# RMS norms around the MLP of a hybrid decoder layer: weight product ahead of the root, part transposes earlier, h read back by plain loads

## The chip, the cores and the metric

The kernel runs on one core of a Trainium2 chip. The core has a matrix engine (TensorE, PE in the rows), a vector engine (VectorE, DVE), an activation engine (ScalarE, ACT), a general engine (GpSimd, POOL) and queues that issue transfers between memory and the on-chip buffer (SyncE's queue is called SPq, GpSimd's own POOLq). The engines run side by side and each works through its own instructions strictly in the order in which they stand; they meet only at semaphores. The metric is the device time of one execution in microseconds (us); lower is better.

## The reference, cut to what matters

```python
def rms_norm(x, w):
    xf = x.astype(jnp.float32)
    y = xf * lax.rsqrt(jnp.mean(xf * xf, axis=-1, keepdims=True) + RMS_EPS)
    return (y * w.astype(jnp.float32)).astype(x.dtype)
...
        mix = jnp.concatenate([o_gdn, o_moba], axis=-1) @ w_out[i]
        h = h + rms_norm(mix, attn_post_norm[i])
        f = jnp.square(jax.nn.relu(rms_norm(h, mlp_pre_norm[i]) @ w_up[i])) @ w_down[i]
        h = h + rms_norm(f, mlp_post_norm[i])
        h = h + jax.nn.sigmoid(h @ w_ple_gate[i]) * (p[i] @ w_ple[i])
```

There are 512 rows of width 1024, and the MLP is 4096 wide. Everything is in 32-bit floats.

## The kernel before

The 512 rows are four tiles of 128 rows (t = 0 to 3). Every large product is made of three matmuls on operands split in a rounded part and a remainder (`mm3`, lines 188 and 191): ACT casts the rounded part ("h" or the first `sr` of a pair), DVE subtracts it for the remainder ("l", or the second `sr`). A weight block goes from a DMA into a slab `sf`, from there by an ACT cast (line 681) and a DVE subtraction (line 682) into two slabs `sr`.

Two places of the program matter here.

The first lies between the attention and the MLP. `po` is the product of the mixed heads with `w_out`, in two halves of 512 columns. The first half of all four tiles is done at once and copied to `h_t[t]` (line 706). The second half is done tile after tile: 24 matmuls for a tile, then its norms. ACT sums the squares of the half (`pn1t`), GpSimd adds the two halves' sums, scales them and takes the power -0.5 (`norm_r`, lines 674, 154 and 155), DVE multiplies by the root and the norm's weight (line 736, two halves) and adds x (line 737, two halves). That is h. ACT sums its squares (`mn0t`, `mn1t`), GpSimd takes the second root, and DVE makes the MLP's input `xr` (line 740). h is stored to memory (`hd`, line 741). PE then transposes `xr` in eight blocks (line 212, names `u`), and ACT and DVE split the result into `u2Th` and `u2Tl` (lines 203 and 204). The transposes of tiles 0 and 1 stand inside the `po` matmuls of tiles 2 and 3. Right behind the `po` of tile 3 come the first products of the MLP, `pu`, on columns 0 to 255, which are tiles 0 and 1; the transposes of tiles 2 and 3 stand inside these.

The second place is the end of the MLP. The last quarter of the down projection (`pd`) is added to sums (`done`, line 904), a norm follows (`qn`, line 909), h is added by an accumulating DMA from GpSimd's queue (line 913; for tile 3 by DVE, line 911), and PE transposes the result (line 892) for the gate product `pg`. Between the two places the MLP keeps PE at work with products of 5 us each.

The order on each engine is made by a scheduler from the order of the code and from ranks; a block under `tc.high_priority(n)` is ranked n places ahead. DMAs issued by the SP queue start in order: one that waits holds those behind it. Slabs are taken from and given back to a list, so the order of `take` and `give` decides which slab a load uses, and with it what it waits for.

Of the kernel before, what the change touches and what calls it, by code (L numbers as in the profile page):

```python
# [12 lines left out]
ALU = mybir.AluOpType  # L13
# [4 lines left out]
NT = T // P  # L18
D = 1024
# [50 lines left out]
def hybrid_layer(ctx: ExitStack, tc: tile.TileContext, x, p, w_in, w_tok, w_out, w_up, w_down, w_ple, w_gate,  # L70
# [33 lines left out]
    def j4(ap):  # L104
        return ap.rearrange("p (j c) -> p j c", j=4)
# [97 lines left out]
        nc.scalar.copy(dst[0], src)  # L203
        nc.vector.tensor_sub(dst[1], src, dst[0].bitcast(F32))  # L204

    def transpose_in(u, dst, t, name):

        for q in range(2):
            pt = ptr(f"{name}{t}_{q}")
            for i in range(4):  # L210
                k = 4 * q + i
                nc.tensor.transpose(pt[:, i * P:(i + 1) * P], u[:, k * P:(k + 1) * P], ident)
            s = (slice(None), slice(4 * q, 4 * q + 4), slice(t * P, (t + 1) * P))
            put_split((dst[0][s], dst[1][s]), j4(pt))


    uT = split_big("uT")
# [453 lines left out]

    def norm_r(ss, name):
        r = m_.tile([P, 1], F32, tag="nr", bufs=4, name=f"{name}r")
        nc.gpsimd.tensor_add(r, ss[:, 0:1], ss[:, 1:2])
        rsqrt(r, r, 1.0 / D, 1)
        return r

    def split(src):
# [24 lines left out]
            out_proj(pts[t], t, k)  # L703
    for t in range(NT):
        pt = pts[t]
        nc.vector.tensor_copy(h_t[t][:, hf(0)], pt)
        sum_half(pt, po_ss[t][:, 0:1], f"pn0{t}")
    wo = load_rows(w_out[:, hf(1)], "wo1", (4, 6, 0, 2))
    xrs = []
# [13 lines left out]
    for t in range(NT):  # L723
        xr = take()
        nc.sync.dma_start(xr, x[tk(t), :])
        pt = pany(f"po1{t}")
        for k in ks:
            out_proj(pt, t, k)
            if t > 1 and k == ks[2 + t]:
                transpose_in(xrs[t - 2], u2T, t - 2, "u2")  # L730
        sum_half(pt, po_ss[t][:, 1:2], f"pn1{t}")
        r = norm_r(po_ss[t], f"pn{t}")
        ss = ss_tile(f"mn{t}")
        for i, src in enumerate((h_t[t][:, hf(0)], pt)):
            hh = h_t[t][:, hf(i)]
            nc.vector.scalar_tensor_tensor(hh, src, r, nw[0][:, hf(i)], op0=ALU.mult, op1=ALU.mult)
            nc.vector.tensor_add(hh, hh, xr[:, hf(i)])
            sum_half(hh, ss[:, i:i + 1], f"mn{i}{t}")
        r = norm_r(ss, f"mn{t}")
        nc.vector.scalar_tensor_tensor(xr, h_t[t], r, nw[1], op0=ALU.mult, op1=ALU.mult)  # L740
        nc.sync.dma_start(hd[tk(t), :], h_t[t])
        give(h_t[t])
        xrs.append(xr)
# [137 lines left out]
    C = ((sums[2], sums[3]), (sums[6], sums[5]))  # L881
    done = [[two(C[t // 2][i])[:, t % 2] for i in range(2)] for t in range(NT)]
    h2T = split_big("h2T")

    h_last = take()
    nc.sync.dma_start(h_last, hd[tk(NT - 1), :])

    def transpose_done(t):
        for q in range(2):
# [6 lines left out]
    for t in range(NT):  # L896
        ss = ss_tile(f"qn{t}")
        for i in range(2):
            pt = pany(f"pd{t}_{i}")
            for n, (r, k) in enumerate((r, k) for r in range(2) for k in range(PAIRS)):  # L900
                mm3(pt, (f_hl[k][0][:, r, tk(t)], f_hl[k][1][:, r, tk(t)]), wd[r, i][k], n == 0, n == 2 * PAIRS - 1)
                if i == 0 and n == 3 and t > 1:
                    transpose_done(t - 2)
            add(done[t][i], done[t][i], pt)
            sum_half(done[t][i], ss[:, i:i + 1], f"qn{i}{t}")

        r = norm_r(ss, f"qn{t}")
        for i in range(2):
            nc.vector.scalar_tensor_tensor(done[t][i], done[t][i], r, nw[0][:, hf(i)], op0=ALU.mult, op1=ALU.mult)
            if t == NT - 1:  # L910
                add(done[t][i], done[t][i], h_last[:, hf(i)])
            else:
                nc.gpsimd.dma_start(done[t][i], hd[tk(t), hf(i)], accum_op=ALU.add)


    late = [nw[0], h_last]
    for i in range(2):
        if i == 1:

# [65 lines left out]
```

## Time and profile before

| | |
|---|---|
| median of 3 runs | 696.54 us (695.7 to 697.95) |
| the profiled execution, its own time | 696.68 us |
| its span, first to last instruction | 694.9 us |
| PE busy | 680.2 us, 98% |
| DVE, ACT, POOL busy | 439.0, 323.8 and 46.5 us |
| bytes read from and written to memory | 70.51 and 7.08 MB |

A row of the timeline gives the start in the span, the duration, the engine, the line, the operation with the tile written and the tiles read, the shape and the count; in brackets stands how long the engine had been idle before it and what ended that. Where several instructions are merged, the duration is from the first start to the last end. An instruction starts somewhat before the one ahead of it has left its engine, so starts lie closer than durations. Durations of matmuls are modelled, their starts are recorded.

### The profile page before, as it was taken

The numbers are of one execution on the slowest core, as the hardware profiler recorded it, in microseconds if no ns is written. First come the engines' busy times: TensorE is split into PE (matmuls) and PEld (weight loads), VectorE is DVE, ScalarE is ACT, GpSimd is POOL, SyncE is SP. The second block draws the span as 40 slices with busy tenths as digits, with TensorE's granted clock in tenths as the row PEclk, the third lists the DMA queues.
The fourth block names the chain that finished last, engine by engine and source line by source line (L and its number), as shares of the span: only waits on it lengthen the run. The fifth ranks groups of instructions, "written<-read, shape, count | busy, mean of one in ns | idle before, by whom it ended". The sixth has DMA issues, their size and how long they took to land.

```text
span 694.9 us, 8996 instructions
## 1 busy us (share of the span) xinstructions
PE 680.2 (98%) x3418; PEld 565.6 (81%) x3418; DVE 439.0 (63%) x689; ACT 323.8 (47%) x598; POOL 46.5 (7%) x89
## 2 busy tenths in 40 slices
PE   8999999999999999979999999999999999999997
PEld 5998888888877768879888888888888888778886
DVE  4748889367676656574476347966579668545632
ACT  6536343433466655345356544644444444532311
POOL 1401100000011100320000000000000000032000
PEclk9999999999999999989999999999999999999999
DMA  8731323532112018368003441054301032644431
GB/s 332 303 122 62 103 86 102 116 110 92 31 31 62 31 62 287 126 211 315 31 31 113 160 134 49 31 160 143 122 31 60 31 121 79 196 105 71 155 109 46
DMA packets 38412, 79.24 MB, mean 114 GB/s; under 512 B 9760, under 2 KB 10400, under 8 KB 38368
## 3 DMA queue, kind: packets, MB, share of 16 engines
q1 hardware_dynamic: 36784, 75.51, 33.4%
q0 software_dynamic: 864, 1.57, 1.6%
q10 hardware_dynamic: 720, 1.57, 0.6%
q8 instruction: 27, 0.44, 0.2%
q14 instruction: 17, 0.14, 0.1%
HBM read 70.51 MB, written 7.08 MB: 112 GB/s over the span
## 4 chain that ended last, share of the span: by engine, by line
PE 88%; DMA 3%; DVE 3%; ACT 3%; issue 2%; POOL 1%; POOLq 0%; ACTq 0%; DVEq 0%
PE pu L191 17%; PE pd L191 13%; PE pu L188 8%; PE pd L188 6%; PE pc L191 6%; PE pg L191 4%; PE pc L188 3%; PE po L191 3%; PE pg L188 2%; PE pmk L191 2%; PE pmq L191 2%; PE wv L191 2%; PE pz L191 2%; PE po L188 1%; PE pav L596 1%
## 5 line engine op out<-in xcount | busy, mean ns | idle before, releaser
L191 PE MATMUL pd<-sr,sr 128*128 128x512 f32 x464 | 143.5, 390 | 0.5 <-DVE sr L682 0.5
L191 PE MATMUL pu<-u2Tl,sr 128*128 128x512 f32 (+1 forms) x288 | 106.2, 369 | 1.7 <-DVE u2Tl L204 1.7
L188 PE MATMUL pu<-u2Th,sr 128*128 128x512 f32 (+1 forms) x288 | 106.0, 370 | 1.9 <-ACT u2Th L203 1.9
L191 PE MATMUL pu<-u2Th,sr 128*128 128x512 f32 (+1 forms) x288 | 106.0, 369 | 0.0
L191 PEld LDWEIGHTS pd<-sr,sr 128*128 128x128 f32 x464 | 86.9, 188 | 19.5 <-DVE sr L682 1.6
L188 PE MATMUL pd<-sr,sr 128*128 128x512 f32 x232 | 90.7, 391 | 0.5 <-ACT sr L681 0.5
L682 DVE TENSOR_TENSOR sr<-sf,sr 128x1024 fp32r<-128x1024 f32 x48 | 58.3, 1221 | 33.8 <-PE pd L191 13.8
L682 DVE TENSOR_TENSOR sr<-wd,sr 128x1024 fp32r<-128x1024 f32 x42 | 51.2, 1221 | 28.5 <-PE pu L191 27.1
L779 ACT ACTIVATE f<-pu 128x512 f32<-128x512 f32 (+1 forms) x36 | 19.9, 551 | 97.9 <-PE pu L191 97.9
L188 PEld LDWEIGHTS pu<-u2Th,sr 128*128 128x128 f32 x288 | 55.1, 192 | 11.1 <-ACT u2Th L203 2.3
L191 PEld LDWEIGHTS pu<-u2Tl,sr 128*128 128x128 f32 x288 | 55.3, 192 | 10.8 <-DVE u2Tl L204 2.0
L191 PEld LDWEIGHTS pu<-u2Th,sr 128*128 128x128 f32 x288 | 55.3, 192 | 8.6
L681 ACT CAST sr<-sf 128x1024 fp32r<-128x1024 f32 x48 | 50.2, 1046 | 25.3 <-DMA sf<-in_w_down 8.9
L681 ACT CAST sr<-wd 128x1024 fp32r<-128x1024 f32 x42 | 44.1, 1050 | 19.4 <-PE pd L191 19.4
L188 PEld LDWEIGHTS pd<-sr,sr 128*128 128x128 f32 x232 | 43.6, 188 | 10.2 <-ACT sr L681 1.3
L188 PE MATMUL pc<-uTh,w_h 128*128 128x512 f32 x96 | 39.0, 407 | 0.0
L191 PE MATMUL pc<-uTh,w_l 128*128 128x512 f32 x96 | 38.4, 400 | 0.0
L191 PE MATMUL pc<-uTl,w_h 128*128 128x512 f32 x96 | 38.2, 398 | 0.0
L833 DVE TENSOR_TENSOR sf<-sf,pd 128x512 f32<-128x512 f32 x28 | 19.0, 683 | 22.2 <-PE pd L191 22.2
L838 DVE TENSOR_TENSOR wd<-wd,wd 128x1024 f32<-128x1024 f32 x24 | 29.3, 1223 | 0.6
L188 PE MATMUL pg<-sr,h2Th 128*128 128x512 f32 (+1 forms) x72 | 26.5, 368 | 0.0
L191 PE MATMUL pg<-sr,h2Th 128*128 128x512 f32 (+1 forms) x72 | 26.3, 366 | 0.0
(422 smaller groups left out, 1318.6 us busy)
## 6 DMA issues: line engine op xcount, KB each, us to landing
sf<-in_w_up SPq DMA_DIRECT2D x32, 512.0 KB, 3.3
wd<-in_w_down SPq DMA_DIRECT2D x24, 512.0 KB, 4.3
w_r<-in_w_in SPq DMA_DIRECT2D x12, 512.0 KB, 3.6
wo_r<-in_w_out SPq DMA_DIRECT2D x8, 512.0 KB, 3.8
sf<-in_w_ple_gate SPq DMA_DIRECT2D x8, 512.0 KB, 3.9
sf<-in_w_down SPq DMA_DIRECT2D x8, 512.0 KB, 4.3
wv_r<-in_w_tok SPq DMA_DIRECT2D x4, 520.0 KB, 6.4
x<-in_x SPq DMA_DIRECT2D x4, 512.0 KB, 6.8
```

Of the source, the lines that this page charges most:

```text
L188: nc.tensor.matmul(dst, l[0], r[0], start=start, stop=False)
L191: nc.tensor.matmul(dst, a, b, start=False, stop=stop and i == 1)
L596: nc.tensor.matmul(po[:, j * P:], mov[:, j, tk(h)], PT[:, j, j * P:], start=j == 0, stop=j == 3)
L681: nc.scalar.copy(hi, src)
L682: nc.vector.tensor_sub(lo, src, hi.bitcast(F32))
L779: nc.scalar.activation(fq[:, side, c0:c1], pt[:, :n], AF.Relu)
L833: add(dst, dst, pts[j])
L838: sub(B[dst + (kk,)], B[x_ + (kk,)], B[y_ + (kk,)])
```

## The change

In `norm_r` GpSimd prepares the sum of the first half ahead, DVE adds the second half's sum to it in one small operation, and GpSimd takes the power. The product with the norm's weight is taken out of the operation that multiplies by the root: it is made from the raw product ahead of the root, for the first half of `po` in place of the copy, and the operation behind the root multiplies by the root and adds x (or h) at once. `xr` is made in two halves. The transposes of tiles 0 and 1 stand one and two steps of three matmuls earlier, and their split parts are ranked 60 places ahead. At the end of the MLP, h is read back for all four tiles by plain loads of 512 KB on the SP queue, and no DMA accumulates. In the changed kernel lines up to 203 keep their numbers; the norm's weight product of the second half stands on line 735, the operation behind the root on 739, `xr` on 743, the small operation of `norm_r` on 676.

```diff
--- before.py
+++ after.py
@@ -203,7 +203,7 @@
         nc.scalar.copy(dst[0], src)
         nc.vector.tensor_sub(dst[1], src, dst[0].bitcast(F32))
 
-    def transpose_in(u, dst, t, name):
+    def transpose_in(u, dst, t, name, ahead=0):
 
         for q in range(2):
             pt = ptr(f"{name}{t}_{q}")
@@ -211,7 +211,8 @@
                 k = 4 * q + i
                 nc.tensor.transpose(pt[:, i * P:(i + 1) * P], u[:, k * P:(k + 1) * P], ident)
             s = (slice(None), slice(4 * q, 4 * q + 4), slice(t * P, (t + 1) * P))
-            put_split((dst[0][s], dst[1][s]), j4(pt))
+            with tc.high_priority(ahead):
+                put_split((dst[0][s], dst[1][s]), j4(pt))
 
 
     uT = split_big("uT")
@@ -671,8 +672,9 @@
 
     def norm_r(ss, name):
         r = m_.tile([P, 1], F32, tag="nr", bufs=4, name=f"{name}r")
-        nc.gpsimd.tensor_add(r, ss[:, 0:1], ss[:, 1:2])
-        rsqrt(r, r, 1.0 / D, 1)
+        nc.gpsimd.tensor_scalar(r, ss[:, 0:1], 1.0 / D, EPS, op0=ALU.mult, op1=ALU.add)
+        nc.vector.scalar_tensor_tensor(r, ss[:, 1:2], 1.0 / D, r, op0=ALU.mult, op1=ALU.add)
+        nc.gpsimd.tensor_tensor(r, r, half[:, :1], op=ALU.pow)
         return r
 
     def split(src):
@@ -703,7 +705,7 @@
             out_proj(pts[t], t, k)
     for t in range(NT):
         pt = pts[t]
-        nc.vector.tensor_copy(h_t[t][:, hf(0)], pt)
+        nc.vector.tensor_mul(h_t[t][:, hf(0)], pt, nw[0][:, hf(0)])
         sum_half(pt, po_ss[t][:, 0:1], f"pn0{t}")
     wo = load_rows(w_out[:, hf(1)], "wo1", (4, 6, 0, 2))
     xrs = []
@@ -726,18 +728,19 @@
         pt = pany(f"po1{t}")
         for k in ks:
             out_proj(pt, t, k)
-            if t > 1 and k == ks[2 + t]:
-                transpose_in(xrs[t - 2], u2T, t - 2, "u2")
+            if t > 1 and k == ks[3]:
+                transpose_in(xrs[t - 2], u2T, t - 2, "u2", 60)
         sum_half(pt, po_ss[t][:, 1:2], f"pn1{t}")
         r = norm_r(po_ss[t], f"pn{t}")
+        nc.vector.tensor_mul(h_t[t][:, hf(1)], pt, nw[0][:, hf(1)])
         ss = ss_tile(f"mn{t}")
-        for i, src in enumerate((h_t[t][:, hf(0)], pt)):
+        for i in range(2):
             hh = h_t[t][:, hf(i)]
-            nc.vector.scalar_tensor_tensor(hh, src, r, nw[0][:, hf(i)], op0=ALU.mult, op1=ALU.mult)
-            nc.vector.tensor_add(hh, hh, xr[:, hf(i)])
+            nc.vector.scalar_tensor_tensor(hh, hh, r, xr[:, hf(i)], op0=ALU.mult, op1=ALU.add)
             sum_half(hh, ss[:, i:i + 1], f"mn{i}{t}")
         r = norm_r(ss, f"mn{t}")
-        nc.vector.scalar_tensor_tensor(xr, h_t[t], r, nw[1], op0=ALU.mult, op1=ALU.mult)
+        for i in range(2):
+            nc.vector.scalar_tensor_tensor(xr[:, hf(i)], h_t[t][:, hf(i)], r, nw[1][:, hf(i)], op0=ALU.mult, op1=ALU.mult)
         nc.sync.dma_start(hd[tk(t), :], h_t[t])
         give(h_t[t])
         xrs.append(xr)
@@ -881,9 +884,9 @@
     C = ((sums[2], sums[3]), (sums[6], sums[5]))
     done = [[two(C[t // 2][i])[:, t % 2] for i in range(2)] for t in range(NT)]
     h2T = split_big("h2T")
-
-    h_last = take()
-    nc.sync.dma_start(h_last, hd[tk(NT - 1), :])
+    h_in = [take() for t in range(NT)]
+    for t in range(NT):
+        nc.sync.dma_start(h_in[t], hd[tk(t), :])
 
     def transpose_done(t):
         for q in range(2):
@@ -906,14 +909,14 @@
 
         r = norm_r(ss, f"qn{t}")
         for i in range(2):
-            nc.vector.scalar_tensor_tensor(done[t][i], done[t][i], r, nw[0][:, hf(i)], op0=ALU.mult, op1=ALU.mult)
-            if t == NT - 1:
-                add(done[t][i], done[t][i], h_last[:, hf(i)])
-            else:
-                nc.gpsimd.dma_start(done[t][i], hd[tk(t), hf(i)], accum_op=ALU.add)
-
-
-    late = [nw[0], h_last]
+            nc.vector.tensor_mul(done[t][i], done[t][i], nw[0][:, hf(i)])
+        for i in range(2):
+            nc.vector.scalar_tensor_tensor(done[t][i], done[t][i], r, h_in[t][:, hf(i)], op0=ALU.mult, op1=ALU.add)
+        if t < NT - 1:
+            give(h_in[t])
+
+
+    late = [nw[0], h_in[NT - 1]]
     for i in range(2):
         if i == 1:
 
```

On PE the transposes of tile 1 (`u_0`, `u_1`, from the slab with tile 1's `xr`) stand inside the `po` of tile 3. Before:

```order
L191 MATMUL po_3012<-wo_6_h,mx3l 128x512
L188 MATMUL po_3012<-wo_0_h,mg0h 128x512
L191 MATMUL po_3012<-wo_0_l,mg0h 128x512
L191 MATMUL po_3012<-wo_0_h,mg0l 128x512
L188 MATMUL po_3012<-wo_0_h,mg1h 128x512
L191 MATMUL po_3012<-wo_0_l,mg1h 128x512
L191 MATMUL po_3012<-wo_0_h,mg1l 128x512
L212 MATMUL u_0_3031<-ident,sf_2659 128x128 x4
L212 MATMUL u_1_3038<-ident,sf_2659 128x128 x4
```

And in the changed kernel:

```order
L188 MATMUL po_3012<-wo_6_h,mx3h 128x512
L191 MATMUL po_3012<-wo_6_l,mx3h 128x512
L191 MATMUL po_3012<-wo_6_h,mx3l 128x512
L212 MATMUL u_0_3025<-ident,sf_2659 128x128 x4
L212 MATMUL u_1_3032<-ident,sf_2659 128x128 x4
L188 MATMUL po_3012<-wo_0_h,mg0h 128x512
```

They moved ahead of six matmuls. Those of tile 0, inside the `po` of tile 2, moved ahead of three.

On DVE, between the `xr` of tile 1 (`sf_2659`) and the split parts of tile 1 (`u2Tl` from `u_0` and `u_1`), the rows before were:

```order
L740 SCALAR_TENSOR_TENSOR sf_2659<-sf_2656,mn1r,sf_2654 128x1024
L204 TENSOR_TENSOR u2Tl<-u_0_2967,u2Th 128x4x128
L204 TENSOR_TENSOR u2Tl<-u_1_2974,u2Th 128x4x128
L736 SCALAR_TENSOR_TENSOR sf_2657<-sf_2657,pn2r,sf_2653 128x512
L736 SCALAR_TENSOR_TENSOR sf_2657<-po_2951,pn2r,sf_2653 128x512
L737 TENSOR_TENSOR sf_2657<-sf_2657,sf_2660 128x512 x2
L682 TENSOR_TENSOR sr_2673<-sf_2663,sr_2672 128x1024
L740 SCALAR_TENSOR_TENSOR sf_2660<-sf_2657,mn2r,sf_2654 128x1024
L204 TENSOR_TENSOR u2Tl<-u_0_3031,u2Th 128x4x128
L204 TENSOR_TENSOR u2Tl<-u_1_3038,u2Th 128x4x128
```

`sf_2657` is h of tile 2, `sf_2660` its `xr`, and `sr_2673` the remainder of a weight block of `w_up` that is loaded into the slab `sf_2663`. In the changed kernel:

```order
L743 SCALAR_TENSOR_TENSOR sf_2659<-sf_2656,mn1r,sf_2654 128x512
L204 TENSOR_TENSOR u2Tl<-u_0_2964,u2Th 128x4x128
L204 TENSOR_TENSOR u2Tl<-u_1_2971,u2Th 128x4x128
L743 SCALAR_TENSOR_TENSOR sf_2659<-sf_2656,mn1r,sf_2654 128x512
L676 SCALAR_TENSOR_TENSOR pn2r<-pn2s,pn2r 128x1
L735 TENSOR_TENSOR sf_2657<-po_2951,sf_2653 128x512
L739 SCALAR_TENSOR_TENSOR sf_2657<-sf_2657,pn2r,sf_2660 128x512 x2
L684 TENSOR_TENSOR sr_2673<-sf_2663,sr_2672 128x1024
L676 SCALAR_TENSOR_TENSOR mn2r<-mn2s,mn2r 128x1
L743 SCALAR_TENSOR_TENSOR sf_2660<-sf_2657,mn2r,sf_2654 128x512
L204 TENSOR_TENSOR u2Tl<-u_0_3025,u2Th 128x4x128
L204 TENSOR_TENSOR u2Tl<-u_1_3032,u2Th 128x4x128
```

The split parts moved between the halves of `xr`. The weight block's remainder stays between the norms of tile 2, and on ACT the order of this stretch is unchanged: sum of squares of `po` of tile 2, cast of the weight block in `sf_2663`, the two sums of squares of h of tile 2, the two casts `u2Th` of tile 1.

On the SP queue, from the load of the last norm's weight on, the loads of the changed kernel stand in this order (`hd` is h, `ple` the embedding's product; before, the slab `sf_3077` took a block of `w_ple_gate`, `sf_2653` and `sf_2654` took parts of `ple`, and behind the last `w_down` block came one load of `hd` and two of `w_ple_gate`):

```order
L889 DMA sf_3077<-hd 128x1024
L692 DMA sf_2659<-in_w_down 128x2x512
L692 DMA sf_2662<-in_w_ple_gate 128x2x512
L692 DMA sf_2653<-in_w_ple_gate 128x2x512
L692 DMA sf_2660<-in_w_down 128x2x512
L932 DMA sf_2662<-ple 128x512
L692 DMA sf_2661<-in_w_down 128x2x512
L692 DMA sf_2659<-in_w_down 128x2x512
L692 DMA sf_2654<-in_w_ple_gate 128x2x512
```

Two blocks of `w_ple_gate` moved from behind the eight `w_down` blocks to between them; the three other loads of `hd` stand where these were.

## Rows read from the trace of the kernel before

**Rows 1.** The page: engines with their busy time (share of the span) and instructions.

```profile
PE 680.2 (98%) x3418; PEld 565.6 (81%) x3418; DVE 439.0 (63%) x689; ACT 323.8 (47%) x598; POOL 46.5 (7%) x89
```

**Rows 2.** Who waited for whom, TensorE's waits: us in total, times, longest.

```profile
PE pu L188 <- ACT u2Th L203: 1.9, 1, 1.9
PE pu L191 <- DVE u2Tl L204: 1.7, 1, 1.7
...
PE pd L188 <- ACT sr L681: 0.5, 1, 0.5
PE pd L191 <- DVE sr L682: 0.5, 1, 0.5
PE h L892 <- DMA sf<-hd: 0.5, 1, 0.5
```

**Rows 3.** Busy time by stretch: length, then PE, PEld, DVE, ACT and POOL busy (instructions), the granted TensorE clock, the DMA engines' share, GB/s.

```profile
236.00:244.00 8.00, 6.58 (x33) 4.85 (x31) 4.64 (x20) 6.11 (x24) 2.40 (x4) 1.00 0.00 1
...
298.00:303.00 5.00, 1.66 (x8) 0.88 (x6) 3.95 (x5) 2.99 (x8) 2.05 (x5) 0.81 0.60 206
303.00:308.00 5.00, 4.69 (x22) 4.69 (x23) 4.51 (x7) 1.77 (x3) 0.55 (x1) 0.51 0.99 336
308.00:312.00 4.00, 4.00 (x36) 4.00 (x36) 1.33 (x2) 2.07 (x5) 0.93 (x3) 1.00 0.41 136
340.00:590.00 250.00, 250.00 (x1105) 206.96 (x1104) 166.74 (x162) 123.23 (x148) 0.00 (x0) 1.00 0.28 88
```

**Rows 4.** The timeline of TensorE, at one wait of an earlier stage and around the end of `po`.

```profile
239.41 0.30 PE L592 MATMUL prt<-ident,pr 128*128 128x128 f32 x1 [1.22 <-DVE pr L589]
...
288.32 0.39 PE L191 MATMUL po<-wo_h,mx3l 128*128 128x512 f32 x1
...
294.66 0.39 PE L191 MATMUL po<-wo_h,mx3l 128*128 128x512 f32 x1
...
298.38 0.40 PE L191 MATMUL po<-wo_h,mg3l 128*128 128x512 f32 x1
300.68 0.89 PE L188 MATMUL pu<-u2Th,sr 128*128 128x256 f32 x4 [1.91 <-ACT u2Th L203]
303.31 0.58 PE L191 MATMUL pu<-u2Tl,sr 128*128 128x256 f32 x1 [1.75 <-DVE u2Tl L204]
...
307.95 0.28 PE L191 MATMUL pu<-u2Tl,sr 128*128 128x256 f32 x1
```

**Rows 5.** The norms of tile 0 on the timelines of ACT, POOL and DVE.

```profile
280.64 0.60 ACT L667 ACTIVATE pn10j<-po 128x512 f32<-128x512 f32 x1 [1.62 <-PE po L191]
...
281.41 0.19 POOL L674 TENSOR_TENSOR pn0r<-pn0s 128x1 f32<-128x1 f32 x1 [38.38 <-ACT pn10j L667]
...
281.97 0.56 POOL L155 TENSOR_TENSOR pn0r<-pn0r,half 128x1 f32<-128x1 f32 x1
...
282.56 0.75 DVE L736 SCALAR_TENSOR_TENSOR sf<-sf,pn0r,sf 128x512 f32<-128x512 f32 x1 [2.44 <-POOL pn0r L155]
...
283.89 1.28 DVE L737 TENSOR_TENSOR sf<-sf,sf 128x512 f32<-128x512 f32 x2
287.38 1.28 DVE L740 SCALAR_TENSOR_TENSOR sf<-sf,mn0r,sf 128x1024 f32<-128x1024 f32 x1 [2.20 <-POOL mn0r L155]
```

**Rows 6.** Small operations of an earlier stage: one on DVE, and the one on POOL that takes its result.

```profile
237.27 0.15 DVE L567 TENSOR_TENSOR so<-so,rq 128x4 f32<-128x4 f32 x1
...
237.59 0.19 POOL L154 TENSOR_SCALAR so<-so 128x4 f32<-128x4 f32 x1 [26.39 <-ACT pr L587]
```

**Rows 7.** From tile 1 to the split parts of tile 1 that the first `pu` reads: rows of ACT, DVE, SPq and POOL.

```profile
286.18 0.60 ACT L667 ACTIVATE pn11j<-po 128x512 f32<-128x512 f32 x1
...
293.81 0.61 ACT L667 ACTIVATE pn12j<-po 128x512 f32<-128x512 f32 x1
...
296.31 1.05 ACT L681 CAST sr<-sf 128x1024 fp32r<-128x1024 f32 x1 [1.80 <-DMA sf<-in_w_up]
298.68 0.63 ACT L667 ACTIVATE mn02j<-sf 128x512 f32<-128x512 f32 x1 [1.32 <-DVE sf L737]
...
299.11 1.21 DVE L682 TENSOR_TENSOR sr<-sf,sr 128x1024 fp32r<-128x1024 f32 x1
301.37 1.28 DVE L740 SCALAR_TENSOR_TENSOR sf<-sf,mn2r,sf 128x1024 f32<-128x1024 f32 x1 [1.05 <-POOL mn2r L155]
302.57 1.28 DVE L204 TENSOR_TENSOR u2Tl<-u,u2Th 128x512 fp32r<-128x512 f32 x2
...
285.20 7.15 SPq L741 DMA_DIRECT2D hd<-sf  x2
292.39 0.44 SPq L718 DMA_DIRECT2D sf<-in_w_up  x1
...
294.59 0.93 POOL L674 TENSOR_TENSOR pn2r<-pn2s 128x1 f32<-128x1 f32 x1 [0.44 <-ACT pn12j L667]
```

**Rows 8.** The page's DMA issues: KB of one, median us from issue to landing.

```profile
sf<-in_w_up SPq DMA_DIRECT2D x32, 512.0 KB, 3.3
...
x<-in_x SPq DMA_DIRECT2D x4, 512.0 KB, 6.8
...
sf<-ple SPq DMA_DIRECT2D x7, 256.0 KB, 2.7
```

**Rows 9.** The timeline of DVE at the end of the MLP: three remainders of `w_down` blocks.

```profile
596.37 3.50 DVE L682 TENSOR_TENSOR sr<-sf,sr 128x1024 fp32r<-128x1024 f32 x3 [4.22 <-PE pu L191]
```

## The prediction

> **What bounds the kernel now.** I read the engines' busy time first: TensorE has work for 98% of the span [rows 1], and through the whole MLP, from 340 to 590 us, it never pauses [rows 3]. So what shortens the kernel is a pause of TensorE, or time that it runs at its lower clock. The list of its waits comes next. Its two longest stand at the first MLP products: 1.9 us for `u2Th` and 1.7 us for `u2Tl`. At the end of the MLP there are three of 0.5 us, two for `w_down` weights and one for the accumulating DMA of h [rows 2]. Then the stretches: between 303 and 308 us the granted clock is 0.51 (the lower level, 1.2 GHz), and 22 matmuls take 5 us, while from 308 us on 36 take 4 us at 1.00 (2.4 GHz), 0.111 us each [rows 3]. TensorE's timeline puts it together: the last matmul of `po` starts at 298.38, so the first `pu` could start 0.23 later, at 298.61 (24 matmuls of `po` and 1 us of transposes lie between 288.32 and 294.66); the 26th `pu` matmul starts at 307.95 [rows 4]. At full clock without a wait, 25 steps of 0.111 bring it at 301.4. About 6.5 us are lost there: the waits, and the clock that fell in them. That is what the change can win at the first place. At the second it is mainly the 0.5 us wait for the DMA.
>
> **The change part by part, first place.** I carry the new order through with the durations of rows, and take 0.1 us for a hand-over that no row shows (rows 5 and 6 show 0.03 to 0.17).
>
> The root. Before: from the first GpSimd operation (281.41) to the DVE operation that uses the root (282.56), 1.15 us [rows 5]. Now: a DVE operation of 0.15, a hand-over of 0.17 [rows 6], the power of 0.56 and 0.03 to DVE [rows 5]: 0.91. The product of `po` with the weight lies under the power; its cost is that of the copy or multiply it replaces. Behind the root two operations replace four: the first half of h is there 0.75 after the root, the second 0.67 later (half the distance of 282.56 and 283.89 [rows 5]).
>
> Tile 0: the sum of squares starts at 280.64 and hands over at 281.41, so 0.77 a sum [rows 5]. Root 282.32, halves of h at 283.07 and 283.74, sums from 283.17 to 284.71, second root 285.62, `xr` in halves at 286.37 and 287.04, in place of 288.66 (287.38 and 1.28 [rows 5]). TensorE reaches the transposes at 288.55, right behind the matmul of 288.32 [rows 4]: no wait.
>
> Tile 1: its `po` sum starts at 286.18 at the latest [rows 7]. Root 287.86, h at 288.61 and 289.28, sums to 290.25, second root 291.16, first half of `xr` 291.91. Now DVE does both split parts of tile 0 (1.28 [rows 7]) before the second half of `xr`, so that is there at 293.8. TensorE wants it behind the matmul of 294.66, at 294.89 [rows 4]: 1.1 us to spare. This cover is thin: if the chain of tile 1 is later by more than that, `po` stalls for the rest.
>
> Tile 2: `po` is done about 292.4. The small operation stands behind the second half of `xr`, 293.8; root 294.7; h at 295.5 and 296.1. On ACT a weight cast stands ahead of the sums of h, and waits for its load. Its issue stands on the SP queue behind the store of h of tile 1, at 292.39 before [rows 7], now near 289.7 (h of tile 1 complete at 289.28; transposes of tile 0 done at 289.6). The load took 3.9 us (292.39 to 296.31 [rows 7]), so it lands at 293.6, the cast ends at 294.65, and the sums start at 295.6, held by h alone, and end at 297.1. On DVE the weight remainder of 1.21 [rows 7] runs to 297.3.
>
> Here one price is uncertain. A GpSimd operation of 0.19 took 0.93 beside a DVE operation on tiles of the buffer [rows 5, 7], so I let GpSimd's preparation of `mn2r` wait until the remainder ends and be done at 297.45: small operation 297.5, root 298.4, first half of `xr` 299.1, first split part of tile 1 at 299.7. The power of `pn1r` and `pn2r` runs beside the product of `po` with the weight (0.64 to 0.69 as the other operations that read `po` or `u` [rows 7]); no row shows that pair. It costs nothing, or, held until the product ends, up to 0.45 each. I take nothing, since the held one of rows 7 stood beside an operation with all inputs in the buffer.
> The Trainium skill (SBUF — State Buffer, Who interferes with whom) states that DVE contends with GpSimd when it has two inputs in SBUF, and not with one input there and one in PSUM. By it the power is not held here, but the weight product at the end of the MLP, with both inputs in SBUF, does hold it; the sum would stay, since a whole tile of `pd` stands between that norm and its transposes.
>
> TensorE therefore starts `pu` at 298.61, its second matmul needs the remainder of tile 1 and starts at 299.8: one wait of 1.2 us instead of 1.9 and 1.7. A wait of 1.22 us at 239.41 left the clock at 1.00 [rows 3, 4]. With the clock kept, the 26th matmul starts at 299.8 and 24 times 0.111, at 302.5 in place of 307.95: 5.5 us won. Tiles 2 and 3 follow a chain of the same shape and TensorE wants them only 36 and 84 `pu` matmuls on, 4 and 9 us later; the weights of the next products were loaded far ahead. From there TensorE is never idle until 590 us, and everything else waits for it, so the 5.5 us stay.
>
> **Second place.** With h read by plain loads, tile 0 needs one operation behind the root instead of that and a DMA; the wait of 0.47 to 0.5 us [rows 2] goes. The three loads of h stand where two `w_ple_gate` loads and one of h stood, behind the last `w_down`, so they land while the products of tiles 1 and 2 still run, ahead of the transposes of tile 0. The two `w_ple_gate` loads moved between the `w_down` loads: some 512 KB more are ahead of the last of these. Cost: nothing if the remainders of `w_down` go on waiting for TensorE, as the three at 596.37 do after 4.2 us of idle DVE [rows 9]; above, 256 KB more cost 0.6 us each (3.3 against 2.7 us to land [rows 8]), so 1.2 us on the two 0.5 us waits for weights. Below nothing: those two could go, a gain of 1.0. I take nothing, being nearest to rows 9. The four more DVE multiplications and the two earlier casts fall where both engines wait for TensorE.
>
> **Sum.** 5.5 and 0.5, 6.0 us: the profiled execution goes from 696.68 to 690.7. It lies 0.1 above the median of 696.54, so I say 690.6.
>
> **Rivals.**
> *The clock falls all the same.* The stretch from 298 us has a clock of 0.81, though TensorE did four matmuls between its waits [rows 3, 4]. So little idle time was enough; against it stands the 1.22 us wait that left the clock alone. The 22 matmuls at half clock took 4.64 us (303.31 to 307.95 [rows 4]) in place of 2.44: 2.2 us are not won, 692.8.
> The Trainium skill (TensorE: Matmul & The Clock Gate, HAM oscillation — how this bites in real kernels) says that a pause for data can throttle TensorE, and that every such pause is paid for again in slow matmuls. Rows 3 agree, 0.51 behind the pause. By it this rival holds if the pause left is still long enough.
> *The weight cast holds the norm (the slower side).* ACT works in order, so the sums of h of tile 2 can't start before the cast of the `w_up` block, and its load now decides as soon as it lands 0.9 us later than worked out (sums ready at 295.6 less the cast's 1.05, 294.5). From there each us costs one. At a landing 4.4 us late, near 298, `u2Tl` is as late as before; with the clock fallen too the place gains nothing, and slower by 0.3% (2.1 us) needs a landing at 300.6, 11 us after the issue. For it: before, ACT stood 1.80 us for this load [rows 7]. Against: the longest median of a 512 KB load is 6.8 us, and of these 3.3 [rows 8]. At 6.8 us the loss is 2.0 us plus the clock's 2.2: 694.8. At 11 us, 698.7 or more.
> *The loads of `w_ple_gate` delay the last `w_down` blocks.* The bound above: 691.8. Against it stand rows 9.
> *Nothing moves.* If DVE, POOL and ACT hand over so slowly that three engines in the root cost what two did, 0.24 us a root comes back. Four roots lie on the path: 691.6, no more.
>
> **How the numbers follow.** My forecast (waits of 0.6 to 1.8 us at `pu`, the clock kept, the second place between 0 and 1 us): 0.62, 689.3 to 691.8. The clock falls: 0.15, 692.8. `w_down` late, or slow roots: 0.08, about 691.7. The cast holds: 0.10, from 692 to 699, of that half above 694.5. Something I have not seen: 0.05. All waits gone at both places would be 688.6. The range is 688.6 to 694.2. A difference of 0.3% (2.1 us) is about what a measurement of this kernel tells from none, so faster ends at 694.4: the first three cases and half of the fourth with some of the fifth, 0.87; same 0.07; slower 0.06.
>
> **What would show it right or wrong.** Right: TensorE's waits list one wait for `u2Tl` of about 1.2 us and none for `u2Th`; the stretch behind it has a clock of 1.00; the weight cast on ACT starts near 293.6 and the sums of tile 2 near 295.6; no transposes wait inside `po`; no wait for h at the end, the two waits for `w_down` still at 0.5. Wrong: a clock near 0.5 behind the first `pu`; a wait of the transposes near 294.9; ACT idle for a DMA ahead of the sums of tile 2; waits for `w_down` above 1 us. If the two places together give less than 2 us, my picture of the first place is wrong.

## The result, and the profile after

The changed kernel takes 690.13 us (median of 5 runs, 689.76 to 690.44) against 696.59 us before (5 runs, 695.70 to 697.95): a ratio of 0.9905, 95% interval 0.9891 to 0.9920. Its profiled execution has a span of 688.1 us, 6.8 us less than the 694.9 of before. Of that, 6.0 us had been forecast. Two executions of the experiments, 2959.63 us of e2_end and 1377.37 us of e5_early, are left out of every time and ratio below.

The page, engines' busy time, to be read against [rows 1]: TensorE is busy for 3.6 us less with the same 3418 instructions. Of this, 2.4 us lie between the last `po` matmul and the first of the last down products (294.3 before, 291.9 after), mainly matmuls that no longer run at half clock; 0.95 lies in the first 20 us (17.86 before, 16.91 after), ahead of the change.

```profile
PE 676.6 (98%) x3418; PEld 563.2 (82%) x3418; DVE 442.6 (64%) x707; ACT 323.7 (47%) x598; POOL 39.3 (6%) x71
```

TensorE's waits after (us in total, times, longest), in place of [rows 2]. The wait for `u2Th` is gone, that for `u2Tl` is 0.5 us, no wait for h is left, and those for `w_down` (line 684 and 683) are still there:

```profile
PE pd L191 <- DVE sr L684: 0.7, 2, 0.5
PE pu L191 <- DVE u2Tl L204: 0.5, 1, 0.5
...
PE pd L188 <- ACT sr L683: 0.3, 1, 0.3
```

The stretches of [rows 3] (length, then PE, PEld, DVE, ACT, POOL busy, granted clock, DMA share, GB/s). The clock is 1.00 throughout, where before it was 0.81 and 0.51:

```profile
298.00:303.00 5.00, 4.53 (x36) 4.18 (x35) 4.94 (x9) 2.81 (x7) 0.73 (x2) 1.00 0.98 317
303.00:308.00 5.00, 5.00 (x45) 5.00 (x44) 3.42 (x6) 2.63 (x6) 1.24 (x2) 1.00 0.98 320
```

TensorE's timeline around the end of `po`, and where the last down products (`pd`) begin, and the transposes behind the first of them, as in [rows 4]. The row at 302.12 is the 26th `pu` matmul:

```profile
298.17 0.39 PE L191 MATMUL po<-wo_h,mg3l 128*128 128x512 f32 x1
298.40 0.28 PE L188 MATMUL pu<-u2Th,sr 128*128 128x256 f32 x1
299.15 0.38 PE L191 MATMUL pu<-u2Tl,sr 128*128 128x256 f32 x1 [0.47 <-DVE u2Tl L204]
299.37 0.28 PE L191 MATMUL pu<-u2Th,sr 128*128 128x256 f32 x1
...
302.12 0.28 PE L191 MATMUL pu<-u2Tl,sr 128*128 128x256 f32 x1
...
590.55 0.39 PE L188 MATMUL pd<-sr,sr 128*128 128x512 f32 x1
...
617.37 1.03 PE L895 MATMUL h<-ident,sf 128*128 128x128 f32 x8
618.15 0.48 PE L188 MATMUL pd<-sr,sr 128*128 128x512 f32 x1
```

And the same last rows before:

```profile
596.34 0.39 PE L188 MATMUL pd<-sr,sr 128*128 128x512 f32 x1
...
624.16 0.63 PE L892 MATMUL h<-ident,sf 128*128 128x128 f32 x4 [0.47 <-DMA sf<-hd]
624.54 0.48 PE L188 MATMUL pd<-sr,sr 128*128 128x512 f32 x1
```

From the last `po` matmul to the first of the last down products it is 292.38 us after and 297.96 before: 5.58 us won at the first place. From there to the matmul behind the transposes 27.60 and 28.20: 0.60 at the second. The last matmul of the program is followed by 4.42 us in place of 4.80 (below), and `po` itself ended 0.21 earlier, for a reason ahead of the change.

The chain of tile 2 that the prediction worked out, on ACT, DVE, POOL and the SP queue, against [rows 7]:

```profile
293.36 1.05 ACT L683 CAST sr<-sf 128x1024 fp32r<-128x1024 f32 x1 [0.35 <-DMA sf<-in_w_up]
295.06 0.63 ACT L668 ACTIVATE mn02j<-sf 128x512 f32<-128x512 f32 x1 [0.65 <-DVE sf L739]
...
292.73 0.74 DVE L743 SCALAR_TENSOR_TENSOR sf<-sf,mn1r,sf 128x512 f32<-128x512 f32 x1
...
295.54 1.22 DVE L684 TENSOR_TENSOR sr<-sf,sr 128x1024 fp32r<-128x1024 f32 x1
296.84 0.16 DVE L676 SCALAR_TENSOR_TENSOR mn2r<-mn2s,mn2r 128x1 f32<-128x1 f32 x1
297.74 0.75 DVE L743 SCALAR_TENSOR_TENSOR sf<-sf,mn2r,sf 128x512 f32<-128x512 f32 x1 [0.74 <-POOL mn2r L677]
298.41 1.28 DVE L204 TENSOR_TENSOR u2Tl<-u,u2Th 128x512 fp32r<-128x512 f32 x2
...
295.94 0.87 POOL L675 TENSOR_SCALAR mn2r<-mn2s 128x1 f32<-128x1 f32 x1 [1.76 <-ACT mn02j L668]
...
289.52 0.33 SPq L720 DMA_DIRECT2D sf<-in_w_up  x1
```

The reader sees two things: ACT's cast no longer decides (h comes 0.65 us behind it), and DVE stands idle for 0.74 us for the root, one operation ahead of the split parts of tile 1 (`u2Tl`) that TensorE waits for.

### The profile page after: what moved, and what is told of

It is laid out like the page before. It is cut to its first block, busy times and chain, and to the rows that moved or that the text cites. A ratio compares the mean times of both kernels' runs of the same rounds, so it can differ in the third digit from the quotient of the medians.

```text
span 688.1 us, 8994 instructions
## 1 busy us (share of the span) xinstructions
PE 676.6 (98%) x3418; PEld 563.2 (82%) x3418; DVE 442.6 (64%) x707; ACT 323.7 (47%) x598; POOL 39.3 (6%) x71
## 4 chain that ended last, share of the span: by engine, by line
PE 88%; DMA 3%; ACT 3%; DVE 3%; issue 1%; POOL 1%; ACTq 0%; DVEq 0%; POOLq 0%
PE pu L191 16%; PE pd L191 14%; PE pu L188 8%; PE pd L188 7%; PE pc L191 6%; PE pg L191 4%; PE pc L188 3%; PE po L191 3%; PE pg L188 2%; PE pmk L191 2%; PE pmq L191 2%; PE wv L191 2%; PE pz L191 2%; DMA sf<-in_w_down 1%; PE po L188 1%; PE pav L597 1%
## 5 line engine op out<-in xcount | busy, mean ns | idle before, releaser
L191 PEld LDWEIGHTS pu<-u2Th,sr 128*128 128x128 f32 x288 | 54.3, 189 | 8.8
L188 PEld LDWEIGHTS pu<-u2Th,sr 128*128 128x128 f32 x288 | 54.3, 189 | 8.6
L188 PE MATMUL pg<-sr,h2Th 128*128 128x512 f32 (+1 forms) x72 | 26.5, 368 | 0.0
L191 PE MATMUL pg<-sr,h2Tl 128*128 128x512 f32 (+1 forms) x72 | 26.3, 366 | 0.0
```

Of the source, the lines that this page charges most:

```text
L188: nc.tensor.matmul(dst, l[0], r[0], start=start, stop=False)
L191: nc.tensor.matmul(dst, a, b, start=False, stop=stop and i == 1)
```

## The experiments

Times are medians beside runs of the kernel before on the same chip. The table gives, from each profiled execution, differences of starts on TensorE's timeline as above: (a) last `po` matmul to the first of the last down products, (b) from there to the matmul behind tile 0's transposes, (c) last matmul to the end of the span.

| kernel | time, us | ratio to before (95%) | a | b | c |
|---|---|---|---|---|---|
| before | 696.6 | | 297.96 | 28.20 | 4.80 |
| changed | 690.13 | 0.9905 (0.9891 to 0.9920) | 292.38 | 27.60 | 4.42 |
| e1_first | 690.08 | 0.9915 (0.9903 to 0.9928) | 292.35 | 27.41 | 4.81 |
| e2_end | 695.07 | 0.9984 (0.9975 to 0.9992) | 297.21 | 27.18 | 4.49 |
| e3_order | 694.37 | 0.9974 (0.9964 to 0.9983) | 294.30 | 27.44 | 4.77 |
| e4_norms | 691.30 | 0.9926 (0.9914 to 0.9938) | 293.06 | 27.90 | 4.50 |
| e8_root | 690.95 | 0.9922 (0.9908 to 0.9935) | 293.58 | 27.33 | 4.44 |
| e12_prod | 692.76 | 0.9943 (0.9929 to 0.9956) | 295.05 | 27.73 | 4.50 |
| e10_early | 689.40 | 0.9898 (0.9885 to 0.9912) | 291.96 | 27.37 | 4.47 |

**One place at a time.** e1_first is the changed kernel with the old end of the MLP; e2_end is the kernel before with the new end (there with its own root). The edit is the last two parts of the diff, undone or done alone:

```diff
-    h_in = [take() for t in range(NT)]
-    for t in range(NT):
-        nc.sync.dma_start(h_in[t], hd[tk(t), :])
+    h_last = take()
+    nc.sync.dma_start(h_last, hd[tk(NT - 1), :])
...
+                nc.gpsimd.dma_start(done[t][i], hd[tk(t), hf(i)], accum_op=ALU.add)
```

> The first place is changed as in the changed kernel; the end of the MLP is as before (accumulating DMA, loads of w_ple_gate in their old places). Theory (the first place carries all but about half a microsecond): from the first pu matmul on as in the changed kernel, one wait of about 0.5 us for u2Tl and a clock of 1.00 behind it; at the end the wait for the accumulating DMA is back, shortened by the shorter root to 0.2 to 0.5 us. Time 690.6, between 690.3 and 691.0. Rival (the loads of h and the order of the w_down loads carry a larger share): 692 or more, with waits for w_down above 0.5 us each.

> Only the end of the MLP is changed: h by plain loads and the weight product ahead of the root there, with the root itself, the norms around po, the transposes and ranks as before. Theory: the two waits of 1.9 and 1.7 us at the first pu and the clock near 0.5 behind them are all there; the wait of 0.5 us for the accumulating DMA is gone; 0.4 to 0.7 us less than before, about 696.0. Rival (end of the MLP gives more): 695 or less. Rival (the moved loads of w_ple_gate delay w_down, hidden in the full change): waits for w_down above 0.5 us each and a time not below before.

e1_first has the time of the changed kernel: its wait for h is gone as well, without the plain loads. e2_end wins 1.5 us by the medians and 1.1 (0.6 to 1.7) by the ratio, more than expected. Its profiled execution is the fastest of its runs (694.64), 2.04 below that of before: 1.02 stand in column b and 0.31 in c, and column a is 0.75 shorter though nothing before the end differs. The two waits at `pu` are there, and only the time at the lower clock is shorter (0.68 against 0.51 in the second row of [rows 3]):

```profile
298.00:303.00 5.00, 1.53 (x8) 0.84 (x6) 3.95 (x6) 2.99 (x8) 2.05 (x5) 0.98 0.61 209
303.00:308.00 5.00, 4.67 (x28) 4.67 (x29) 4.53 (x7) 2.06 (x5) 0.55 (x2) 0.68 0.96 330
```

So the price of the fallen clock is not the same in every execution, and part of this gain is that. The accumulating DMAs of tile 0 were issued as follows, first in before, then in e3_order below, whose end is the same; in both that is 21.3 us behind the start of column b (596.34 and 594.06):

```profile
617.66 1.98 POOL L913 DMA_DIRECT2D sf<-hd  x2 [1.11 <-DVE sf L909]
```

```profile
615.37 1.99 POOL L914 DMA_DIRECT2D sf<-hd  x2 [1.11 <-DMA sf<-ple]
...
620.71 1.03 PE L893 MATMUL h<-ident,sf 128*128 128x128 f32 x8
```

In before the first four transposes started 5.43 us behind the first issue, and the last four then waited 0.47 us. In e3_order all eight run without a wait from 5.34 us behind it on, although nothing at its end was changed: the 0.47 us of [rows 2] came and went with how long that DMA took.

**The order alone, and the norms alone.** e3_order adds the following to the kernel before, with the block under `tc.high_priority(ahead)` that the change has in `transpose_in`; e4_norms takes the same order and rank out of the changed kernel:

```diff
-            if t > 1 and k == ks[2 + t]:
-                transpose_in(xrs[t - 2], u2T, t - 2, "u2")
+            if t > 1 and k == ks[3]:
+                transpose_in(xrs[t - 2], u2T, t - 2, "u2", 60)
```

> Only the order is changed: transposes of tiles 0 and 1 earlier, their split parts ranked 60 places ahead; norms and end of the MLP as before. Theory (the order alone does most, because the split parts of tile 1 no longer stand behind the norms of tile 2): the transposes of tile 1 now wait for xr, about 1.6 us inside po (xr of tile 1 ready near 296.5, wanted at 294.9), and pu waits another 0.5 us for u2Tl; with the clock kept about 2.3 us are lost in place of 6.5, time 692.3; if the clock falls behind the waits 694.5. Rival (the norms' chain is the whole matter, and transposes moved ahead of an unchanged chain only move the wait): 696 to 698, with a wait of over 3 us in po.

> The changed kernel with the old places of the transposes of tiles 0 and 1 and without the rank for their split parts. Theory: the norms' chain alone gives about 5 us at the first place; the split parts of tile 1 stand behind the whole xr of tile 2, 0.67 us later than in the changed kernel, so one wait for u2Tl of about 1.1 us, the clock kept at 1.00, time 690.8. Rival (a wait of about 1.1 us at this place lowers the clock): granted clock near 0.5 in the microseconds behind it and a time of 692.5 to 693.3. Rival (the order carries the gain): waits as before and 694 or more.

TensorE's timeline of e3_order, its waits from `po` on:

```profile
296.34 1.06 PE L212 MATMUL u<-ident,sf 128*128 128x128 f32 x8 [1.08 <-issue]
...
301.35 0.38 PE L191 MATMUL pu<-u2Tl,sr 128*128 128x256 f32 x1 [0.66 <-DVE u2Tl L204]
...
315.93 0.39 PE L191 MATMUL pu<-u2Tl,sr 128*128 128x256 f32 x1 [0.99 <-DVE u2Tl L204]
```

The order alone wins 2.2 us and keeps the clock (1.00 in both stretches), as the theory said, but 2 us less than expected. The waits in `po` and at `pu` are near their forecast (1.1 and 0.7 for 1.6 and 0.5); the last one, for the split parts of tile 3, was not in it: with the old norms tile 3 comes late too. That is 1 us; of the rest 0.8 is that the profiled execution took 693.6, less than the median.

e4_norms keeps the clock at 1.00 behind a wait of the length that I had forecast for the changed kernel, and is 1.2 us slower than that kernel, 0.67 of it in this wait and 0.3 in column b. All of the change but the order thus wins 5.3 us on the kernel before:

```profile
300.05 0.39 PE L191 MATMUL pu<-u2Tl,sr 128*128 128x256 f32 x1 [1.14 <-DVE u2Tl L204]
```

```profile
298.00:303.00 5.00, 3.86 (x29) 3.48 (x28) 4.67 (x8) 1.59 (x6) 0.55 (x1) 1.00 0.82 269
303.00:308.00 5.00, 5.00 (x45) 5.00 (x44) 3.58 (x6) 3.94 (x8) 0.74 (x2) 1.00 0.93 339
```

**The two parts of the norms.** e8_root puts the old root into the changed kernel; e12_prod takes back, together, the product ahead of the root around `po` and the halves of `xr`:

```diff
-        nc.gpsimd.tensor_scalar(r, ss[:, 0:1], 1.0 / D, EPS, op0=ALU.mult, op1=ALU.add)
-        nc.vector.scalar_tensor_tensor(r, ss[:, 1:2], 1.0 / D, r, op0=ALU.mult, op1=ALU.add)
-        nc.gpsimd.tensor_tensor(r, r, half[:, :1], op=ALU.pow)
+        nc.gpsimd.tensor_add(r, ss[:, 0:1], ss[:, 1:2])
+        rsqrt(r, r, 1.0 / D, 1)
```

```diff
-        nc.vector.tensor_mul(h_t[t][:, hf(1)], pt, nw[0][:, hf(1)])
...
-            nc.vector.scalar_tensor_tensor(hh, hh, r, xr[:, hf(i)], op0=ALU.mult, op1=ALU.add)
+            nc.vector.scalar_tensor_tensor(hh, src, r, nw[0][:, hf(i)], op0=ALU.mult, op1=ALU.mult)
+            nc.vector.tensor_add(hh, hh, xr[:, hf(i)])
```

> The changed kernel with the old root (GpSimd adds, scales and takes the power; no DVE operation). Theory (each root on the path costs about 0.3 us: 1.15 before, 0.84 measured in the changed kernel): the two roots of tile 1 push DVE's work on tile 2 about 0.6 us later, and GpSimd's first operation of the second root of tile 2 stands behind the weight remainder; wait for u2Tl about 1.1 us instead of 0.47, clock kept, time 690.8. Rival (the slack on the way takes the roots in): the wait stays at 0.5 and the time at 690.1. Rival (GpSimd is held at several places): wait of 2 us or more and 692.

> The changed kernel without the weight product ahead of the root around po and without xr in halves: copy of the first half of po, two multiplications and two additions behind the root, xr whole; the new root, order and end of the MLP stay. Theory (four operations behind the root instead of two are worth 1.2 to 1.4 us): xr of tile 1 is later by about 1.9 us than in the changed kernel, past the 1.3 us it had to spare, so the transposes of tile 1 wait about 0.5 us in po, pu waits 0.6 to 0.9 us for u2Tl, and another 0.4 us behind tile 3; time 691.5. Rival (order and root do it all, the operations behind the root are hidden): 690.1 to 690.4 and no wait in po.

e8_root: 0.8 us slower than the changed kernel, its wait for `u2Tl` 1.36 in place of 0.47. The roots lie on the path, and the slack on the way does not take them in. e12_prod: 2.6 us slower. Its waits are

```profile
295.56 1.07 PE L212 MATMUL u<-ident,sf 128*128 128x128 f32 x8 [0.53 <-issue]
299.55 0.38 PE L188 MATMUL pu<-u2Th,sr 128*128 128x256 f32 x1 [0.17 <-ACT u2Th L203]
300.60 0.38 PE L191 MATMUL pu<-u2Tl,sr 128*128 128x256 f32 x1 [0.67 <-DVE u2Tl L204]
314.54 0.38 PE L188 MATMUL pu<-u2Th,sr 128*128 128x256 f32 x1 [0.57 <-ACT u2Th L203]
315.91 0.38 PE L191 MATMUL pu<-u2Tl,sr 128*128 128x256 f32 x1 [0.99 <-DVE u2Tl L204]
```

2.93 us in all, 2.46 more than the 0.47 of the changed kernel, which is its loss. The first three are what was expected; behind tile 3 it is 1.56 where I had said 0.4. The product ahead of the root, with `xr` in halves, is the largest part of the change that was tried by itself, and half of what it brings lies with tile 3. Which of the two brings how much was not tried.

**Longer waits at the same place, and the clock.** e6_hold1 and e7_hold2 compute half of `u2Tl` of tile 1 once or twice more; e9_hold3 computes it four times, the last time late:

```diff
             with tc.high_priority(ahead):
                 put_split((dst[0][s], dst[1][s]), j4(pt))
+                if ahead and (t, q) == (1, 0):
+                    for _ in range(1):
+                        nc.vector.tensor_sub(dst[1][s], j4(pt), dst[0][s].bitcast(F32))
```

> The changed kernel with one remainder of tile 1 (half of u2Tl) computed a second time behind the two, so that TensorE's wait at the second pu matmul grows from 0.47 to about 1.7 us, about as long as each of the two waits before, but alone. Theory (the clock falls only behind the pair of waits with four matmuls between): granted clock 1.00 behind it, time 1.2 us above the changed kernel, 691.3. Rival (one pause of this length is enough): granted clock near 0.5 in the following microseconds as in rows of before, 1.4 to 2.2 us more, 692.8 to 693.5.

> As the run with one more remainder, but with two, and half of xr of tile 2 between them: one wait of about 2.9 us at the second pu matmul. Theory (only the pair of waits lowers the clock): granted clock 1.00, time 2.5 us above the changed kernel, 692.6. Rival (a single pause of nearly 3 us lowers it): granted clock near 0.5 behind it, 694.0 to 694.9.

> The changed kernel with half of u2Tl of tile 1 computed four times, the last time behind the weight product of tile 3 on DVE: TensorE does two matmuls, four transposes and two matmuls while it waits some 0.9 and 2.5 us for u2Tl, in all nearly as long as before (1.9 and 1.7 us). Theory (the clock falls behind about 3.5 us of waits with little between, and holds at up to 1.9): granted clock near 0.5 in the microseconds behind, 3.8 us of delay and 1.4 to 2.2 for the clock, 695.3 to 696.1. Rival (the clock holds here too, so that before it fell for a reason other than the length of the waits): granted clock 1.00 and 693.9.

(e7_hold2 has `range(2)`; e9_hold3 makes three copies ahead of the last one.) The first two missed their aim: the scheduler put transposes of tile 2 and other `pu` matmuls into the gap, so that the one long wait became 0.95 us ahead of three transposes (e6_hold1, 690.87 us) or 0.94 and 0.96 (e7_hold2, 692.79). The clock stayed at 1.00, which says nothing of a single long pause. e9_hold3 came closer to the kernel before:

```profile
300.69 0.66 PE L212 MATMUL u<-ident,sf 128*128 128x128 f32 x4 [0.95 <-DVE u2Tl L204]
301.10 0.48 PE L188 MATMUL pu<-u2Th,sr 128*128 128x256 f32 x2
303.81 0.39 PE L191 MATMUL pu<-u2Tl,sr 128*128 128x256 f32 x1 [2.23 <-DVE u2Tl L219]
```

```profile
298.00:303.00 5.00, 2.63 (x15) 1.99 (x13) 4.31 (x8) 2.66 (x5) 0.93 (x3) 1.00 0.98 312
303.00:308.00 5.00, 4.18 (x35) 4.19 (x36) 4.33 (x8) 1.83 (x5) 0.93 (x3) 1.00 1.01 366
```

With 0.95 and 2.23 us of waits, four transposes and two matmuls between them, the clock is still 1.00. That is 3.18 us in all, 0.5 less than the 3.66 of before, so the run did not quite reach what it was made for: my theory on what lowers the clock is not borne out, but not refuted either. The time doesn't decide, though 694.37 us is nearer to the rival's 693.9 than to my 695.3, because tile 3 came late as well, with two more waits that neither had counted:

```profile
316.77 0.39 PE L188 MATMUL pu<-u2Th,sr 128*128 128x256 f32 x1 [0.37 <-ACT u2Th L203]
318.15 0.39 PE L191 MATMUL pu<-u2Tl,sr 128*128 128x256 f32 x1 [0.99 <-DVE u2Tl L204]
```

The four waits are 4.54 us, 4.07 more than the 0.47 of the changed kernel; at full clock that makes 694.2, beside the 694.37 measured. In the profiled executions the clock fell at this place only behind the pair of 1.91 and about 1.8 us (before and e2_end). What makes that pair different stays open. The length of one wait does not settle it: 2.23 us left the clock at 1.00 here, and an early stage has 0.59 behind 2.06 (last section).

**The wait that is left.** e5_early and e10_early are one kernel: the changed one with the transposes of tile 1 three matmuls earlier still. e5_early left no profile to compare, so it ran again beside e11_after, the changed kernel unaltered.

```diff
-            if t > 1 and k == ks[3]:
+            if t > 1 and k == ks[5 - t]:
```

> The changed kernel with the transposes of tile 1 three matmuls earlier in the po of tile 3. The scheduler then puts the split parts of tile 1 on DVE ahead of the second root's small operation of tile 2 and its xr, and on ACT between the two sums of tile 2. Theory (the wait of 0.47 us left at the second pu matmul is a matter of DVE's order alone, since DVE stands idle for 0.74 us for the root just ahead): xr of tile 1 is ready at 293.5 and TensorE wants it at 294.1, so no wait in po; no wait at pu either, as the first split part is done near 297.4; xr of tile 2 is ready near 300, as before; 0.4 to 0.5 us less than the changed kernel, 689.65. Rival (the second sum of tile 2, now about 1 us later behind the casts, makes the wait reappear at the transposes of tile 2): 690.1 or more, with a wait of the transposes inside the first pu products.

> The same kernel as e5_early once more, for its profile: no wait for u2Tl at pu, none in po and none at the transposes of tile 2; 0.4 to 0.5 us less than the changed kernel run beside it. Rival: the wait reappears at the transposes of tile 2 or 3, no difference.

> The changed kernel once more, on the same chip as e10_early, as its partner: 690.1, one wait of 0.5 us for u2Tl, clock 1.00.

e5_early: ratio to before 0.9906 (0.9891 to 0.9921), which cannot be told from the changed kernel's. e10_early: 689.40 us (689.29 to 689.83) beside 690.19 (689.66 to 690.92) of e11_after. Its profile has no wait at `pu`. DVE does the split parts ahead of the small operation of the second root, 1.75 us earlier than in the changed kernel (298.41), and its wait for the root, 0.67 us, now stands behind them, where TensorE does not feel it:

```profile
296.66 1.28 DVE L204 TENSOR_TENSOR u2Tl<-u,u2Th 128x512 fp32r<-128x512 f32 x2
297.86 0.15 DVE L676 SCALAR_TENSOR_TENSOR mn2r<-mn2s,mn2r 128x1 f32<-128x1 f32 x1
298.68 1.42 DVE L743 SCALAR_TENSOR_TENSOR sf<-sf,mn2r,sf 128x512 f32<-128x512 f32 x2 [0.67 <-POOL mn2r L677]
```

Column a is 0.42 shorter, as expected. The medians are 0.8 apart; the rest is e11_after's early stage, as far as its profile tells (last section): its four runs are 690.63 and 690.92 at a mean granted clock of 0.997 and 0.996, and 689.66 and 689.75 at 0.999 and 1.000. This version is the fastest of all, by its trace for the reason given, while the two times by themselves are close to what runs scatter.

## Why the prediction came out

**First place, 5.5 us: right in size, with two terms that were off and mostly cancelled.** To the 26th `pu` matmul it is 9.57 us from the last `po` before and 3.95 after, 5.62 won. From the first `pu` matmul to the second I had 1.19 us; it is 0.75 (298.40 to 299.15), of which the list of waits counts 0.47, below the 0.6 to 1.8 that I had set for my case. The chain of tile 2 was 0.3 to 0.7 earlier at its steps, 0.2 of it because `po` itself ended 0.21 earlier: the root took 0.84 (281.34 to 282.18 on DVE) and not 0.91, the second half of `xr` of tile 1 was done at 293.47 and not 293.8, the small operation of the second root stood at 296.84 and not 297.5. Against that, the step of the `pu` matmuls is 0.12 (299.37 to 302.12 in 23 steps), not 0.111: I had divided the stretch from 308 to 312 us in [rows 3] by a count that holds the matmuls cut by its edges. So the 24 steps behind the wait took 2.97 us and not 2.66, which gave back 0.3 of the 0.44, and makes the slow clock's price of before about 2.0 and not 2.2. That the two nearly cancel is luck.

**The clock: kept, as forecast.** 1.00 in both stretches. e4_norms shows that it would have been kept with the longer wait too. The rival of 692.8 fails. The Trainium skill (TensorE: Matmul & The Clock Gate, HAM oscillation — how this bites in real kernels) stood behind that rival: it has a kernel whose every wait for data throttles TensorE again. The pair of waits of before agrees (0.51 behind it). The single waits of 0.47, 1.14 and 1.36 us at this place were followed by 1.00, so not every wait is paid for in this way.

**The weight cast: not in the way.** Its load was issued at 289.52 (forecast 289.7), landed for the cast at 293.36 (forecast 293.6), and the sums waited 0.65 us for h behind it. The slower rival needed a landing 0.9 us late; there were 0.65 left.

**No stall in `po`.** Tile 1's `xr` was done at 293.47, wanted at 294.79: 1.3 us to spare where I had 1.1. e12_prod shows how thin that is: with four operations behind the root it turns into a wait.

**GpSimd beside DVE.** The preparation of `mn2r` was held to the end of the weight remainder, as worked out (0.87 in place of 0.19). The disputed pair is now in the trace: the power beside the product that reads `po`, and beside the one at the end of the MLP whose inputs are both in the buffer.

```profile
281.42 0.69 DVE L735 TENSOR_TENSOR sf<-po,sf 128x512 f32<-128x512 f32 x1
...
281.59 0.56 POOL L677 TENSOR_TENSOR pn0r<-pn0r,half 128x1 f32<-128x1 f32 x1 [6.60 <-DVE pn0r L676]
...
607.47 0.68 DVE L912 TENSOR_TENSOR sf<-sf,sf 128x512 f32<-128x512 f32 x1
...
607.63 0.93 POOL L677 TENSOR_TENSOR qn0r<-qn0r,half 128x1 f32<-128x1 f32 x1 [4.68 <-DVE qn0r L676]
```

The first is not held (0.56), the second ends 0.4 us behind the product (0.93), and TensorE does not wait for it there. By the rule of the Trainium skill (SBUF — State Buffer, Who interferes with whom) it had to be so, and the trace agrees in both.

**Second place, 0.5 us: the size came out, by luck.** 0.60 was measured in column b. But the step "the wait of 0.47 to 0.5 us goes" with the plain loads was a reading of one execution: e3_order has the accumulating DMA and the old root and no such wait, and e1_first, without plain loads, has column b at 27.41 and the time of the changed kernel (690.08). Column b lies between 27.18 and 27.90 in every kernel but before, whatever its end. So the plain loads bring nothing that shows on top of the first place; the 1.1 us of e2_end, against the kernel before, are in part its shorter time at the lower clock and for the rest not explained. The waits for `w_down` stay, as said (0.19, 0.33 and 0.52 after; 0.15, 0.32 and 0.49 in e1_first, with the `w_ple_gate` loads in their old places), so these loads cost next to nothing.

**The chances.** They do not add up as I wrote them: my first three cases are 0.85 and half of the fourth 0.05, so faster is 0.90 or more by them, and not 0.87.

**How the parts add up.** Taken out of the changed kernel one at a time, the product costs 2.6 us, the order 1.2, the root 0.8 and the end nothing: 4.6, less than the 6.5 of all. Put in alone, the order already keeps the clock and wins 2.2, and the end wins 1.1 to 1.5. Norms without the order (e4_norms) and the order without the norms (e3_order) both keep the clock, so its price, some 2 us, is saved by whichever is there and shows in neither loss. With it the sum is 6.6; that the waits add up in this way is worked out from these sizes and was not tried pair by pair.

## What to carry to other kernels

Where an engine in order feeds the one that bounds, look for its idle time just ahead of the work that is waited for: putting that work ahead of the gap (a root's 0.7 us) brought 0.42 us here, where the shorter roots bring 0.8, and costs an earlier transposition. Carry the chain through to the last tile and not just to the first: the old norms (e3_order) or the old products (e12_prod) made TensorE wait 1 to 1.6 us for tile 3 when tile 1 had been mended. A wait of half a microsecond for a DMA in one profile is no term of a sum until a second execution shows it.

## What the runs showed of the hardware that I had not expected

The lower clock also comes in an early stage, in some executions of the same kernel. Window and wait of TensorE from 18 us on, first in the changed kernel's profile, then in e11_after's:

```profile
18.00:22.00 4.00, 3.65 (x27) 3.06 (x26) 3.27 (x5) 3.75 (x7) 0.93 (x3) 1.00 1.06 406
...
17.56 1.09 PE L212 MATMUL ut<-ident,u 128*128 128x128 f32 x8 [1.47 <-DVE u L268]
```

```profile
18.00:22.00 4.00, 4.00 (x18) 3.42 (x18) 3.13 (x4) 3.10 (x6) 0.73 (x2) 0.59 1.06 406
...
17.91 1.27 PE L212 MATMUL ut<-ident,u 128*128 128x128 f32 x8 [2.06 <-DVE u L268]
```

In the second TensorE had waited 2.06 us for `u` just ahead, and the clock behind it is 0.59; `po` then ended at 299.12 and not 298.17; of these 0.95 us, 0.35 lie ahead of the transposes (17.91 and 17.56) and 0.60 behind them. e6_hold1 and e9_hold3 show the same (waits of 2.05 and 2.02, clock 0.58 and 0.62). Over the thirteen profiles that can be compared, the wait at this spot is 0.62 to 1.86 us in ten, with a clock of 1.00 from 18 to 22 us, and 2.02 to 2.06 us in these three. That is up to 1 us of scatter that no edit here has to do with, and about as much as the end of the MLP wins on the kernel before.

Column c: from the last matmul to the end of the span it is 4.77 to 4.81 us in the three kernels of the table with accumulating DMAs from GpSimd's queue (before, e1_first, e3_order), and 4.42 to 4.50 in the six without. The work behind the last matmul is the same in both. It is 0.3 us that I had not counted; the reason was not tried.
